# The gate of a modulation in a two-block mixer: sums on VectorE in place of matmuls

## The chip, the core and the metric

The kernel runs on one core of a Trainium2 chip. Its engines are TensorE (PE; its weight loads are listed as PEld), VectorE (DVE), ScalarE (ACT), GpSimd (POOL) and SyncE (SP), whose queue issues most DMAs. Each engine works through its own row of instructions in order and waits on semaphores for the others. The metric is the device time of one execution in microseconds. Of the kernel before there are three runs: 3599.32, 3597.35 and 3597.96 us, the median 3597.96.

## The reference, cut to what matters

Two blocks follow each other over 512 tokens of width D = 2048. The first one starts with a modulation of its input by a vector `c` and ends with a gate; between them are an attention and a state-space scan (SSD) over 512 tokens and 256 context tokens, which share one input projection `w_in`.

```
shift, scale, gate = split(silu(c) @ w_mod + b_mod, 3)        # w_mod: 2048 x 6144
px = (rmsnorm(x) * (1 + scale) + shift) @ w_in                 # the context likewise, from c_ctx
...                                                            # attention, scan, norms
x = x + gate * (merged @ w_out)
```

The context is not updated, so of its own modulation only shift and scale are used; the gate third of `w_mod` (2048 x 2048, 16 MB in fp32) is needed for `c` alone. The gate is first read when the output projection `w_out` is added to x, long after the scan. Everything is fp32 to the outside.

## The kernel before

**Main product.** An activation and a weight are each split in a high and a low half (fp32r), and a product is the sum of three matmuls, high-high, low-high, high-low. `weights` loads a `raw` tile of two rows of 128 (three buffers), `split` makes `wh` on ScalarE (a cast) and `wl` on VectorE (a subtraction), each with two buffers, and `block` runs the matmuls into PSUM tiles `acc`. A step is one such pair of rows; a product over D has eight steps.

**Stages of the first block.** `block1` loads c and c_ctx, makes `cs` (silu of both in the first 2 of 32 columns, per row of 128), then shift and scale by `mod`, in which `cs` is the stationary operand and a tile `wm` of 512 columns of `w_mod` streams; the two column groups of 512 and the two parities of k go to four different groups of 32 PSUM partitions. `sel` then sums them and puts the result on partitions. `ssd` runs four groups g (`ssd_group`): the columns of x (`xa`, `xb`, `xc`; 256 columns of `w_in`), of B and C (`ba`, `ca`, `bc`; 128 and 128), the convolution (`conv3`, tiles `P`, `u`, `uB`, `uC`), the states S and four chunks of the scan (`A`, `E`, `W`, `y`). `gate_half` is called after groups 1 and 2; it calls `mod` for two strips of 512 gate columns each, with 32 loads of 256 KB in a pool of two buffers per tag (`ss2`), and adds the bias. `keys` follows in the same pools, and then `heads`.

**What sets the order.** The code is written in the order of the computation; a scheduler with a timeline of its own sets each engine's row. `weights` stands under a high priority (`ahead` = 4000 in this stage), so steps of the main product are drawn forward between the other work; the gate's instructions have the ordinary priority and fill in. All DMAs named here are issued by SP in one row. A load into a pool's buffer is issued only when the last reader of that buffer is done, and what stands behind it in SP's row waits too.

Of the kernel before, what the change touches and what calls it, by code (L numbers as in the profile page):

```python
# [8 lines left out]
F32 = mybir.dt.float32  # L9
# [3 lines left out]
ALU = mybir.AluOpType  # L13
# [4 lines left out]
D = 2048  # L18
NX = 512
NCTX = 256  # L20
KT = 16
# [72 lines left out]
class Kernel:  # L94
# [171 lines left out]
    def block1(self):  # L266
        tc, nc, a = self.tc, self.nc, self.a
# [3 lines left out]
        wm = a["w_mod"][0]  # L271
# [6 lines left out]
        cs = [self.four(F32).rearrange("p j (s t) -> p (j s) t", s=2)]  # L278
        with self.pool("lead", 1) as lead, self.pool("lead2", 2) as lead2, self.pool("lead3", LX) as lead3, self.pool("wm", LM) as wmp:
# [10 lines left out]
            ps = self.psm()  # L290
# [1 line left out]
            cc = self.t(lead, [128, 32], F32, "cc")  # L292
            self.act(cc, ps[:, 0:32], AF.Tanh, scale=0.5)
            self.ts(cc, cc, 0.5, ALU.mult, 0.5, ALU.add)
            self.cs = self.t(self.b1, [128, KT, 32], F32, "cs")
            nc.vector.memset(self.cs, 0.0)
            self.tt(self.cs[:, :, 0:2], cc.rearrange("p (s k) -> p k s", s=2),
                    ps[:, 0:32].rearrange("p (s k) -> p k s", s=2), ALU.mult)
            s = self.t(lead, [128, 6, 4], F32, "s")


            for i in range(6):
                for q in range(4):
# [3 lines left out]
                    ps = self.psm()  # L307
# [22 lines left out]
            ps = self.psm()  # L330
            self.spread(ps, r[:, 0:4], 4)
            nc.vector.tensor_copy(rx[:, 0:NX], ps)
            ps = self.psm()
# [17 lines left out]
            for fg in range(4):  # L351
                m = ahead.pop()
                h4, e4, l4 = self.four(F32R), self.four(F32R), self.four(F32R)
                for j in range(4):
                    k = fg * 4 + j
                    sc = self.t(lead2, [128, 2], F32, "sc")
                    sh = self.t(lead2, [128, 2], F32, "sh")
                    q = self.q1["b_mod"]
                    self.ts(sh, m[:, j, 0:2], self.p1[:, q + k:q + k + 1], ALU.add)
                    self.ts(sc, m[:, j, 2:4], self.p1[:, q + KT + k:q + KT + k + 1], ALU.add, 1.0, ALU.add)  # L360
                    q = self.q1["norm_g"]
# [52 lines left out]
    def ssd(self):  # L414
        tc, nc, a = self.tc, self.nc, self.a
        w_in = a["w_in"][0]
        self.ysd = self.t(self.dr, [8, 128, NX], F32, "ysd")
        opx = self.zx
        opc = self.zc
        with ExitStack() as es:  # L420
            p1 = es.enter_context(self.pool("ssc", 1))

            dtT = self.t(p1, [128, 6, 64], F32, "dtT")
            ath = self.t(p1, [128, 6, 32], F32, "ath")
            atl = self.t(p1, [128, 6, 32], F32, "atl")
            ex = self.t(p1, [128, 6, 96], F32, "ex")
            wd = self.t(p1, [128, 6, 32], F32, "wd")
            dsk = self.t(p1, [128, 16], F32, "dsk")
            nc.sync.dma_start(out=dsk, in_=a["d_skip"][0:1, :].to_broadcast([128, 16]))
            pp = es.enter_context(self.pool("pp", 4))  # L430
            xa, xb, ba, ca, xc, bc = self.p0
            first = [self.padded(pp, xa, xc[:, 0:256]), self.padded(pp, xb, xc[:, 256:512]),
                     self.padded(pp, ba, bc[:, 0:256]), self.padded(pp, ca, None)]
            self.psum_pools(4, 4)
            with self.pool("dt", 1) as pd:
                w = self.dtw
                bias = self.t(pd, [32, 2], F32, "dtb")
                for i, (n, m) in enumerate((("dt_bias_f", "a_log_f"), ("dt_bias_b", "a_log_b"))):
                    nc.sync.dma_start(out=bias[i * 16:i * 16 + 16, 0:1], in_=a[n][0].rearrange("(h o) -> h o", o=1))
                    nc.sync.dma_start(out=bias[i * 16:i * 16 + 16, 1:2], in_=a[m][0].rearrange("(h o) -> h o", o=1))  # L440
                pre = self.t(pd, [32, NX + NCTX], F32, "dtpre")
                for ops, at, n in ((opx, 0, NX), (opc, NX, NCTX)):
                    ps = self.acc()
                    for k in range(KT):
                        self.mm(ps[0:64, 0:n], w[:, k, :], ops[k][0], start=(k == 0), stop=False)
                        self.mm(ps[0:64, 0:n], w[:, k, :], ops[k][1], start=False, stop=(k == KT - 1))
                    self.act(pre[:, at:at + n], ps[0:32, 0:n], AF.Identity, bias=bias[:, 0:1])
                    self.tt(pre[:, at:at + n], pre[:, at:at + n], ps[32:64, 0:n], ALU.add)
                st = self.t(pd, [64, NX + NCTX], F32, "dtst")
                self.softplus(pd, st[0:32, :], pre)  # L450
                self.act(bias[:, 1:2], bias[:, 1:2], AF.Exp)
                self.ts(st[32:64, :], st[0:32, :], bias[:, 1:2], ALU.mult, -1.0, ALU.mult)
                for i in range(2):
                    ps = self.psm()
                    for j in range(3):
                        tk = (i * 3 + j) * 128
                        self.tr(ps[:, j * 64:j * 64 + 64], st[:, tk:tk + 128])
                    nc.vector.tensor_copy(dtT[:, i * 3:i * 3 + 3, :], ps[:, 0:192].rearrange("p (j f) -> p j f", j=3))
                atr = self.t(pd, [128, 6, 32], F32R, "atr")
                nc.vector.tensor_copy(atr, dtT[:, :, 32:64])  # L460
                nc.vector.tensor_copy(ath, atr.bitcast(F32))
            self.dt_pool.__exit__(None, None, None)
            self.tt(atl, dtT[:, :, 32:64], ath, ALU.subtract)
            for i in range(2):
                ps = self.psm()
                for j in range(3):
                    t = i * 3 + j
                    o = j * 96
                    self.mm(ps[:, o:o + 16], self.le, dtT[:, t, 32:48])
                    self.mm(ps[:, o + 16:o + 32], self.ge, dtT[:, t, 48:64])  # L470
                    self.mm(ps[:, o + 32:o + 48], self.gt, dtT[:, t, 32:48])
                    self.mm(ps[:, o + 48:o + 64], self.lt, dtT[:, t, 48:64])
                    self.mm(ps[:, o + 64:o + 96], self.ones, dtT[:, t, 32:64])
                self.act(ex[:, i * 3:i * 3 + 3, :], ps[:, 0:288].rearrange("p (j f) -> p j f", j=3), AF.Exp)
            self.tt(wd, dtT[:, :, 0:32], ex[:, :, 32:64], ALU.mult)
            q = self.q1["conv_w0"]
            self.ts(self.p1[:, q:q + 64], self.p1[:, q:q + 64], 0.5, ALU.mult)
            with self.pool("ss1", 1) as s1, self.pool("ss2", 2) as s2, self.pool("ss4", 3) as self.p4:
                for g in range(4):
                    self.ssd_group(g, first if g == 0 else None, pp, s1, s2, dtT, ath, atl, ex, wd, dsk)  # L480
                    if g in (1, 2):
                        self.gate_half(g - 1, s1, s2)
                self.keys(pp)


# [173 lines left out]
            nc.scalar.copy(t[:, 0:512], vs[i])  # L659
            nc.sync.dma_start(out=self.vd[2 * i:2 * i + 2].rearrange("i p c -> p i c"), in_=t[:, 0:512].rearrange("p (i c) -> p i c", i=2))  # L660

    def gate_half(self, fg, pool, raws):
        q = self.q1["b_mod"] + 32
        m = self.mod(self.a["w_mod"][0], pool, [2 * D + fg * 1024, 2 * D + fg * 1024 + 512], raws, 1, self.nc.sync)
        for i in range(2):
            o = fg * 8 + i * 4
            self.tt(self.gate[:, o:o + 4], m[:, :, 2 * i], self.p1[:, q + o:q + o + 4], ALU.add)

    def heads(self):
        tc, nc, a = self.tc, self.nc, self.a  # L670
# [1198 lines left out]
```

## Time and profile before

| what | value |
|---|---|
| profiled execution | 3597.96 us |
| its span, first to last instruction | 3596.1 us |
| mean granted TensorE clock | 0.985 of full speed |
| PE busy | 3507.5 us (98%) |
| DVE busy | 2173.8 us (60%) |
| ACT busy | 1368.8 us (38%) |
| mean DMA rate | 123 GB/s |

The gate's matmuls lie between 262 and 523 us from the start of the span. A group of the page names a line, an engine, an operation and what it writes and reads (`acc<-wm,cs` is a matmul into `acc` from `wm` and `cs`). Lines of helpers (L112 for every matmul, L122 for every operation of two tensors, L132 for the fused multiply-add) stand for many places, so the tile names tell them apart. A matmul with fp32 operands leaves two records.

### The profile page before, as it was taken

The page shows a single profiled execution, that of the slowest core. Times are in us where ns is not written, and L with a number is a line of the kernel's source. Part 1 is how long each engine was busy: PE and PEld are TensorE (multiplying, and loading weights), DVE is VectorE, ACT ScalarE, POOL GpSimd, SP SyncE. Part 2 cuts the span into 40 slices and gives each one's busy share as a digit, 9 for nine tenths or more (in the row PEclk, how much of TensorE's full clock was granted, in tenths as well). Part 3 has the DMA queues.
Part 4 walks back from the last instruction along what each step waited for, and adds up shares of the span by engine and source line. Part 5 has one row for each costly group of instructions (what it writes and reads, how often), then busy time and mean ns, then how long its engine had stood idle before and what let it go on. Part 6 is the DMA issues. An engine that isn't in the chain of part 4 may idle for free.

```text
span 3596.1 us, 48583 instructions
## 1 busy us (share of the span) xinstructions
PE 3507.5 (98%) x18850; PEld 2748.8 (76%) x18850; DVE 2173.8 (60%) x3432; ACT 1368.8 (38%) x2225; POOL 55.7 (2%) x50
## 2 busy tenths in 40 slices
PE   6899999999999999999999998999999999999998
PEld 3486668777778788788877786888888888788887
DVE  3364555456554545675466557777788788555445
ACT  3333443356533323443233334444444444322212
POOL 0000000000000000000000000000000000000000
PEclk8999999999999999999999999999999999999999
DMA  8813333322144353334444443334443344534333
GB/s 278 283 36 112 99 100 88 95 67 82 48 138 147 107 149 109 112 116 116 132 121 129 145 141 129 117 117 127 131 122 107 118 123 141 187 122 126 99 100 106
DMA packets 352602, 442.22 MB, mean 123 GB/s; under 512 B 45871, under 2 KB 200179, under 8 KB 351731
## 3 DMA queue, kind: packets, MB, share of 16 engines
q1 hardware_dynamic: 349456, 437.82, 39.9%
q8 instruction: 148, 2.42, 0.3%
q10 hardware_dynamic: 2915, 1.29, 0.1%
q14 instruction: 83, 0.68, 0.1%
HBM read 383.45 MB, written 55.57 MB: 122 GB/s over the span
## 4 chain that ended last, share of the span: by engine, by line
PE 93%; DMA 3%; DVE 2%; ACT 1%; issue 0%; SPq 0%; POOL 0%; DVEq 0%; ACTq 0%; POOLq 0%
PE acc L112 44%; PE psm L112 23%; PE pp L112 23%; PE psm L116 2%; DMA wm<-in_w_mod_dram 1%; PE pt L116 1%; DVE wl L122 0%; DMA xr<-in_x_dram 0%; DMA raw<-in_ffn_w_down_dram 0%; DMA ym<-ysd 0%; DVE op L122 0%; PE acc L116 0%; DMA xr<-in_ctx_dram 0%; DMA fr<-in_ffn_w_up_dram 0%; DVE s L122 0%
## 5 line engine op out<-in xcount | busy, mean ns | idle before, releaser
L112 PE MATMUL acc<-op,wh 128*128 128x512 f32 (+2 forms) x4160 | 1254.5, 390 | 14.8 <-DVE sl L132 4.6
L112 PEld LDWEIGHTS acc<-op,wh 128*128 128x128 f32 (+1 forms) x4160 | 764.1, 189 | 229.5 <-issue 54.9
L122 DVE TENSOR_TENSOR wl<-raw,wh 128x512 fp32r<-128x512 f32 (+4 forms) x464 | 421.0, 908 | 690.0 <-ACT wh L136 641.1
L112 PE MATMUL acc<-op,wl 128*128 128x512 f32 (+2 forms) x2080 | 773.0, 389 | 2.1 <-DVE wl L122 2.1
L136 ACT CAST wh<-raw 128x512 fp32r<-128x512 f32 (+4 forms) x464 | 369.1, 796 | 1028.3 <-PE acc L112 637.7
L112 PE MATMUL pp<-wh,op 128*128 128x512 f32 x2112 | 529.9, 393 | 10.2 <-ACT wh L136 10.1
L136 ACT CAST wh<-fr 128x1024 fp32r<-128x1024 f32 x308 | 323.1, 1052 | 402.0 <-PE pp L112 350.2
L112 PEld LDWEIGHTS acc<-op,wl 128*128 128x128 f32 (+1 forms) x2080 | 390.4, 189 | 108.7 <-issue 26.9
L112 PEld LDWEIGHTS pp<-wh,op 128*128 128x128 f32 x2112 | 397.4, 188 | 99.3 <-ACT wh L136 10.7
L122 DVE TENSOR_TENSOR wl<-fr,wh 128x1024 fp32r<-128x1024 f32 x308 | 371.1, 1220 | 100.5 <-ACT wh L136 65.5
L112 PE MATMUL psm<-wh,op 128*128 128x512 f32 x1280 | 396.2, 391 | 7.3 <-DVE facc L122 7.3
L112 PEld LDWEIGHTS psm<-wh,op 128*128 128x128 f32 x1280 | 241.4, 189 | 58.2 <-issue 7.7
L112 PE MATMUL pp<-wl,op 128*128 128x512 f32 x1056 | 285.3, 392 | 0.2 <-DVE wl L122 0.2
L112 PE MATMUL psm<-wl,op 128*128 128x512 f32 x640 | 250.1, 391 | 0.3 <-DVE wl L122 0.3
L122 DVE TENSOR_TENSOR fr<-fr,fr 128x1024 f32<-128x1024 f32 x176 | 211.1, 1220 | 50.9 <-DMA fr<-in_ffn_w_gate_dram 33.0
L112 PEld LDWEIGHTS pp<-wl,op 128*128 128x128 f32 x1056 | 197.9, 188 | 43.6 <-DVE wl L122 0.6
L122 DVE TENSOR_TENSOR facc<-facc,psm 128x512 f32<-128x512 f32 x176 | 118.0, 686 | 60.6 <-PE psm L112 54.2
L112 PEld LDWEIGHTS psm<-wl,op 128*128 128x128 f32 x640 | 120.7, 189 | 25.7 <-DVE wl L122 0.7
L112 PE MATMUL acc<-wm,cs 128*32 128x512 f32 x384 | 126.1, 616 | 11.8 <-DMA wm<-in_w_mod_dram 11.8
L112 PE MATMUL acc<-wh,op 128*128 128x256 f32 x576 | 114.8, 293 | 0.0
L112 PEld LDWEIGHTS acc<-wh,op 128*128 128x128 f32 x576 | 91.9, 192 | 5.2 <-issue 3.8
L112 PE MATMUL pp<-wh,opx 128*128 128x512 f32 x352 | 93.8, 399 | 0.0
(469 smaller groups left out, 3506.0 us busy)
## 6 DMA issues: line engine op xcount, KB each, us to landing
raw<-in_w_in_dram SPq DMA_DIRECT2D x216, 256.0 KB, 2.8
fr<-in_ffn_w_gate_dram SPq DMA_DIRECT2D x88, 512.0 KB, 4.1
fr<-in_ffn_w_up_dram SPq DMA_DIRECT2D x88, 512.0 KB, 4.0
raw<-in_ffn_w_down_dram SPq DMA_DIRECT2D x88, 512.0 KB, 3.8
wm<-in_w_mod_dram SPq DMA_DIRECT2D x64, 512.0 KB, 5.8
raw<-in_w_out_dram SPq DMA_DIRECT2D x64, 512.0 KB, 3.8
raw<-in_w_in_dram SPq DMA_DIRECT2D x240, 128.0 KB, 2.4
wm<-in_w_mod_dram SPq DMA_DIRECT2D x64, 256.0 KB, 2.8
```

The source lines that it names most:

```text
L112: self.nc.tensor.matmul(out, lhsT=l, rhs=r, start=start, stop=stop, skip_group_check=more)
L116: self.nc.tensor.transpose(out, x, self.ident[0:n, 0:n])
L122: (e or self.nc.vector).tensor_tensor(out=out, in0=x, in1=y, op=op)
L136: self.nc.scalar.copy(h, x)
```

## The change

The gate third is no longer multiplied on TensorE. `gate_part(i)` makes one strip of 512 gate columns and is called after each of the four groups of the scan. Per row of 128 (k = 0 to 15) it loads a `wm` tile of 128x512 and multiplies it on VectorE by the silu of c for that row, a scalar per partition (`cv`), adding to an accumulator `ga` in SBUF: the first by `tensor_scalar`, fifteen by `scalar_tensor_tensor`. Then four matmuls with `ga` as the stationary operand and a column of ones sum over the 128 partitions, which also puts the result on partitions, and the bias is added straight from PSUM. `cs` moves to the pool of the leading stage, and `cv` (16 columns) stays in its place; the `wm` tiles have a pool `gw` of their own, with two buffers as before.

```diff
-            self.cs = self.t(self.b1, [128, KT, 32], F32, "cs")
+            self.cs = self.t(lead, [128, KT, 32], F32, "cs")
+            self.cv = self.t(self.b1, [128, KT], F32, "cv")
...
+            nc.vector.tensor_copy(self.cv, self.cs[:, :, 0])
...
-            with self.pool("ss1", 1) as s1, self.pool("ss2", 2) as s2, self.pool("ss4", 3) as self.p4:
+            with self.pool("ss1", 1) as s1, self.pool("ss2", 2) as s2, self.pool("ss4", 3) as self.p4, self.pool("gw", 2) as gw:
                 for g in range(4):
                     self.ssd_group(g, first if g == 0 else None, pp, s1, s2, dtT, ath, atl, ex, wd, dsk)
-                    if g in (1, 2):
-                        self.gate_half(g - 1, s1, s2)
+                    self.gate_part(g, s1, gw)
...
-    def gate_half(self, fg, pool, raws):
+    def gate_part(self, i, pool, raws):
+        nc = self.nc
         q = self.q1["b_mod"] + 32
-        m = self.mod(self.a["w_mod"][0], pool, [2 * D + fg * 1024, 2 * D + fg * 1024 + 512], raws, 1, self.nc.sync)
-        for i in range(2):
-            o = fg * 8 + i * 4
-            self.tt(self.gate[:, o:o + 4], m[:, :, 2 * i], self.p1[:, q + o:q + o + 4], ALU.add)
+        acc = self.t(pool, [128, 512], F32, "ga")
+        c0 = 2 * D + i * 512
+        for k in range(KT):
+            w = self.t(raws, [128, 512], F32, "wm")
+            nc.sync.dma_start(out=w, in_=self.a["w_mod"][0][k * 128:(k + 1) * 128, c0:c0 + 512])
+            s = self.cv[:, k:k + 1]
+            if k == 0:
+                self.ts(acc, w, s, ALU.mult)
+            else:
+                self.stt(acc, w, s, acc, ALU.mult, ALU.add)
+        ps = self.psm()
+        for j in range(4):
+            self.mm(ps[:, j:j + 1], acc[:, j * 128:j * 128 + 128], self.ones[:, 0:1])
+        o = i * 4
+        self.tt(self.gate[:, o:o + 4], ps[:, 0:4], self.p1[:, q + o:q + o + 4], ALU.add)
```

The scheduler lays the rows anew from the second gate load on to the first heads (PE's rows agree again from there to the end). Numbers of tiles differ between the two kernels, since they count all tiles made: `wl_2084` before is `wl_2144` now, 60 later. Three places:

VectorE in the first group of the scan, before: the low halves `wl`, `wd` and `XW` of the scan, the additions in `W`.

```order
L122 TENSOR_TENSOR W_1681<-le_1324,dtT_1345 128x512
L122 TENSOR_TENSOR W_1681<-W_1681,y_1682 128x512
L122 TENSOR_TENSOR wd_1349<-dtT_1345,ex_1348 128x192
L122 TENSOR_TENSOR wl_2084<-raw_2081,wh_2083 128x2x256
L122 TENSOR_TENSOR XW_1610<-XB_1545,wd_1349 128x256 x2
L122 TENSOR_TENSOR wl_2167<-raw_2163,wh_2166 128x2x256
```

The same place now (of the products 1880 to 1898, seven in a row, two stand):

```order
L127 TENSOR_SCALAR ga_1873<-wm_1874,cv_117 128x512
L122 TENSOR_TENSOR W_1686<-W_1686,y_1687 128x512
L132 SCALAR_TENSOR_TENSOR ga_1873<-wm_1877,cv_117,ga_1873 128x512
L132 SCALAR_TENSOR_TENSOR ga_1873<-wm_1880,cv_117,ga_1873 128x512
...
L132 SCALAR_TENSOR_TENSOR ga_1873<-wm_1898,cv_117,ga_1873 128x512
L122 TENSOR_TENSOR wd_1351<-dtT_1347,ex_1350 128x192
L132 SCALAR_TENSOR_TENSOR ga_1873<-wm_1901,cv_117,ga_1873 128x512
L132 SCALAR_TENSOR_TENSOR ga_1873<-wm_1904,cv_117,ga_1873 128x512
L122 TENSOR_TENSOR wl_2144<-raw_2141,wh_2143 128x2x256
L132 SCALAR_TENSOR_TENSOR ga_1873<-wm_1907,cv_117,ga_1873 128x512
```

The first product stands ahead of the addition in `W`, ten more between that addition and the low half that came two rows behind it.

VectorE at the second strip, now, from the low half of the last wide step of group 1 on; `P` copies belong to the next group's convolution:

```order
L122 TENSOR_TENSOR wl_2991<-raw_2988,wh_2990 128x2x256
L132 SCALAR_TENSOR_TENSOR ga_2720<-wm_2727,cv_117,ga_2720 128x512
L132 SCALAR_TENSOR_TENSOR ga_2720<-wm_2730,cv_117,ga_2720 128x512
L122 TENSOR_TENSOR XW_2462<-XB_2183,wd_1351 128x256 x2
L132 SCALAR_TENSOR_TENSOR ga_2720<-wm_2733,cv_117,ga_2720 128x512
L132 SCALAR_TENSOR_TENSOR ga_2720<-wm_2736,cv_117,ga_2720 128x512
L122 TENSOR_TENSOR wl_3074<-raw_3070,wh_3073 128x2x256
L132 SCALAR_TENSOR_TENSOR ga_2720<-wm_2739,cv_117,ga_2720 128x512
L132 SCALAR_TENSOR_TENSOR ga_2720<-wm_2742,cv_117,ga_2720 128x512
L132 SCALAR_TENSOR_TENSOR ga_2720<-wm_2745,cv_117,ga_2720 128x512
L505 COPY P_3018<-acc_2777 128x256
```

Two or three products stand between two low halves; further on in the strip one or two, between the 769-column operations of the convolution.

SP in the first group, before, loads of 128-column pieces (two DMAs each) and the third gate load:

```order
L146 DMA raw_2188<-in_w_in_dram 128x2x128 x2
L146 DMA raw_2213<-in_w_in_dram 128x2x128 x2
L146 DMA raw_2238<-in_w_in_dram 128x2x128 x2
L146 DMA raw_2263<-in_w_in_dram 128x2x128 x2
L949 DMA wm_2667<-in_w_mod_dram 128x512
L146 DMA raw_2288<-in_w_in_dram 128x2x128 x2
```

and now (of eleven gate loads in a row, three stand):

```order
L146 DMA raw_2248<-in_w_in_dram 128x2x128 x2
L671 DMA wm_1880<-in_w_mod_dram 128x512
L671 DMA wm_1883<-in_w_mod_dram 128x512
...
L671 DMA wm_1910<-in_w_mod_dram 128x512
L146 DMA raw_2273<-in_w_in_dram 128x2x128 x2
L671 DMA wm_1913<-in_w_mod_dram 128x512
```

Eleven gate loads, each waiting for a buffer, stand where one load of the main product followed the other.

## Rows read from the trace of the kernel before

**Rows 1.** The page's busy shares by engine, and its chain by engine.

```profile
PE 3507.5 (98%) x18850; PEld 2748.8 (76%) x18850; DVE 2173.8 (60%) x3432; ACT 1368.8 (38%) x2225; POOL 55.7 (2%) x50
PE 93%; DMA 3%; DVE 2%; ACT 1%; issue 0%; SPq 0%; POOL 0%; DVEq 0%; ACTq 0%; POOLq 0%
```

**Rows 2.** Busy time by stretch: the gate's stretch, then one without gate matmuls.

```profile
core 0: us, PE busy (x) PEld busy (x) DVE busy (x) ACT busy (x) POOL busy (x), PEclk, DMA share, GB/s
254.00:523.00 269.00, 269.00 (x1198) 173.19 (x1196) 140.84 (x292) 100.32 (x261) 0.00 (x0) 1.00 0.36 104
523.00:600.00 77.00, 77.00 (x488) 67.11 (x487) 46.83 (x96) 37.99 (x107) 0.00 (x0) 1.00 0.23 63
```

**Rows 3.** Groups of PE in 254 to 523 us: the gate's matmuls (busy, mean ns).

```profile
L112 PE MATMUL acc<-wm,cs 128*32 128x512 f32 x128 | 63.8, 605 | 0.0
```

**Rows 4.** Timeline of PE: start, duration, instruction; main product, single gate matmuls, two together.

```profile
308.02 0.39 PE L112 MATMUL acc<-op,wl 128*128 128x512 f32 x1
308.25 0.62 PE L112 MATMUL acc<-op,wh 128*128 128x512 f32 x2
...
302.94 1.04 PE L112 MATMUL acc<-wm,cs 128*32 128x512 f32 x2
303.92 0.38 PE L112 MATMUL acc<-op,wl 128*128 128x256 f32 x1
...
290.42 1.05 PE L112 MATMUL acc<-wm,cs 128*32 128x512 f32 x4
```

**Rows 5.** Waits in 260 to 620 us: all engines, then SP's queue (total, times, longest).

```profile
ACT wh L136 <- PE acc L112: 116.7, 33, 7.0
...
SPq L949 <- PE acc L112: 143.2, 55, 5.5
SPq L146 <- DVE wl L122: 92.1, 27, 7.9
```

**Rows 6.** Timeline of PE: two small matmuls after each other.

```profile
237.18 0.39 PE L112 MATMUL psm<-dtT,ones 128*128 128x32 f32 x2
237.40 0.37 PE L112 MATMUL psm<-dtT,le 128*128 128x16 f32 x2
```

**Rows 7.** DVE: groups in 254 to 523 us, then two starts from the timeline.

```profile
L122 DVE TENSOR_TENSOR XW<-XB,wd 128x256 f32<-128x256 f32 x28 | 10.8, 419 | 19.1 <-ACT XB L530 10.3 <-PE psm L112 8.9
L132 DVE SCALAR_TENSOR_TENSOR u<-P,p,u 128x769 f32<-128x769 f32 x12 | 11.7, 1014 | 0.0
L132 DVE SCALAR_TENSOR_TENSOR uC<-P,p,uC 128x512 f32<-128x512 f32 x4 | 3.0, 742 | 0.0
...
304.15 0.74 DVE L132 SCALAR_TENSOR_TENSOR uC<-P,p,uC 128x512 f32<-128x512 f32 x1
304.82 0.68 DVE L122 TENSOR_TENSOR E<-E,W 128x512 f32<-128x512 f32 x1
```

**Rows 8.** DMA: gate loads (KB, median us to landing), their spread, lead-stage loads.

```profile
wm<-in_w_mod_dram SPq DMA_DIRECT2D x62, 256.0 KB, 2.7
DMA to landing us min/median/max: 2.6/2.7/3.2
...
wm<-in_w_mod_dram SPq DMA_DIRECT2D x64, 512.0 KB, 5.8
```

**Rows 9.** Timeline where strip 1 comes to stand: DVE, then PE.

```profile
233.28 0.69 DVE L122 TENSOR_TENSOR W<-W,y 128x512 f32<-128x512 f32 x1
243.66 0.36 DVE L122 TENSOR_TENSOR wd<-dtT,ex 128x192 f32<-128x192 f32 x1 [9.69 <-ACT ex L119]
246.31 0.69 DVE L122 TENSOR_TENSOR wl<-raw,wh 128x512 fp32r<-128x512 f32 x1 [2.29 <-ACT wh L136]
...
250.38 0.40 PE L112 MATMUL acc<-op,wl 128*128 128x512 f32 x1
```

**Rows 10.** Busy time by stretch: the granted clock (before the DMA share).

```profile
238.00:249.00 11.00, 11.00 (x51) 10.42 (x51) 1.05 (x2) 2.16 (x6) 0.00 (x0) 0.53 0.07 17
```

## The prediction

> **What bounds the kernel now.** I read the page's busy shares and its chain first: TensorE (PE) is busy 98% of the span and makes up 93% of the chain that ended last [rows 1]. A share over the whole span says nothing on one stage, so next I cut out the stage that the change touches. The gate's matmuls run from 262 to 523 us; in 254 to 523 us PE is busy all of the 269.00 us, at full clock, while VectorE (DVE) works 140.84 us, ScalarE 100.32 us, and the DMA share is 0.36 [rows 2]. Then the groups of that stretch: 128 records (64 matmuls, two records each) of `acc<-wm,cs` hold 63.8 us [rows 3]. "Busy" may hide pipelining, so I read the timeline for pitches, start to start. A 128x512 matmul of the main product follows its neighbour after 0.23 us (308.02, 308.25), so the main work goes at its usual pitch with no hole. A gate matmul at 302.94 holds PE until 303.92: 0.98 us [rows 4]. Last the waits: DMA issues of `wm` waited 143.2 us for PE, and the high half `wh` on ScalarE 116.7 us for PE [rows 5]. Everything waits for PE, PE for nothing. So in this stretch a microsecond taken from PE is one from the kernel, as long as nobody else becomes late.
>
> **The change part by part.** The profiled execution took 3597.96 us, 1.86 over its span of 3596.1, and is itself the median of the three runs; I count from it.
>
> (a) Removed from PE: the 64 gate matmuls. In the timeline of the stretch they stand in 61 places: 58 alone, as at 302.94, and three times two together (290.42, four records, 1.05 us) [rows 4]. The 61 pitches lie at 0.97 or 0.98, so 61 x 0.977 = 59.6 us. Also gone are the eight `sel` matmuls of 4 columns and, on ScalarE, two row copies. Small matmuls of this kind stand 0.22 apart (237.18 to 237.40) [rows 6]; 8 x 0.22 = 1.8 us.
>
> A rule of the Trainium skill speaks against so full a price. "Perfetto Trace Analysis", section Identifying the Most-Contended Engine, says that matmul busy share is no measure of headroom and that the share of weight loads is; by that, 173.19 of 269 us [rows 2] would leave a third of PE free, and an estimate by that page has only two thirds of the 59.6 us come back, 39 us; the sum below would end near 3573 us. The pitches of [rows 4] speak for the full price, and I keep it.
>
> (b) Added to PE: 16 matmuls with a column of ones, 16 x 0.22 = 3.5 us by the same row. PE's sum: 59.6 + 1.8 - 3.5 = 57.9 us less.
>
> (c) Added to DVE: 64 products on 128x512, 60 of them fused multiply-adds. The nearest row is the `uC` one, 742 ns, starting 0.67 us before the next instruction (304.15 to 304.82) [rows 7]. 64 x 0.67 = 43 us. With 140.84 us now in the stretch [rows 2] that is 184 us in 269 - 58 = 211 us, 87%: it fits, with little to spare. The four additions of 4 columns take the place of four like them, and the copies of 16 columns become one instead of two; I take 0 for these.
>
> (d) Moved: who waits for the gate's loads. Their number and size stay (64 of 256 KB), but DVE is now the engine that waits, and it runs its row in order; behind it are the low halves `wl`, without which PE stops at the third matmul of a step. `gw` has two buffers: a load lands 2.7 us after its issue [rows 8], its product takes 0.67, and only then can the load after next be issued. So two loads per 2.7 + 0.67 + about 0.1 = 3.45 us. The loads also stand in SP's queue in front of the main product's `raw` loads; three `raw` buffers are ahead of that.
>
> Strip 1 by the order: after the addition at 233.28 [rows 9] come nine products that wait on landings, and then `wl_2144`, the one that stood as `wl_2084` at 246.31. The first of these landings follows a release at 233.75: five rounds of 3.45 from there give 251.0, and the subtraction of 0.69 ends near 252.0 instead of 247.0. PE first reads it at 250.38 [rows 9]: 1.6 us of stall. That row also gives the cushion, 250.38 - 247.0 = 3.4 us, which a low half has before PE needs it.
>
> Strip 2, from `wl_2991` to `wl_3174`: DVE's row holds 11 products (7.4 us), five subtractions (3.1), twelve operations on 256 columns (4.1, at 419 ns less the overlap) and eight on 769 (6.6, at up to 1014) [rows 7]: 21.2 us. Its first seven products are paced by landings, 3.5 x 3.45 = 12.1 us against 7.3 us of work there, so add 4.8: 26.0 us. PE's matmuls between the same two points, at 0.23 us per 512 columns and half that for 256, with the small ones between, come to 20.6 us. DVE falls 5.4 us back, the cushion takes 3.4, 2.0 are left; as some low halves are already late when the strip begins, I take 3. Strips 3 and 4 have the same loads, fewer wide operations beside them, and steps of 3.5 to 5.9 us of PE: counted likewise some 4.7 us of lag each, 1.3 past the cushion; I take 2 each. Strips: 1.6 + 3 + 2 + 2 = 8.6 us. Bounds: 0 (PE's row has other work ahead) and, with landings of 3.2 us, the longest of this size [rows 8], 7 rounds x 0.5 x 4 strips = 14 more, 22.6.
>
> (e) Between the strips lie the chunks of the scan, whose steps go from ScalarE to PE to DVE and back. With PE's gate matmuls gone they have less cover. From 523 to 600 us there are chunks and no gate matmuls, and PE is busy 77.00 of 77.00 us [rows 2]: cover enough. Bounds 0 and 8 us; I take 3.
>
> Sum: 57.9 - 8.6 - 3 = 46.3 us. 3597.96 - 46.3 = **3552 us**. What comes after the scan keeps its order and simply starts earlier.
>
> **The rivals.**
> 1. All covered: the strips' waits fit under PE's row and the cushion. For it: PE waits for nothing now, and a cushion of 3.4 us stands at each step. Against it: the counts of strips 2 to 4. 3597.96 - 57.9 = 3540 us.
> 2. The clock falls in the strips. The stretch 238 to 249 us was granted 0.53, nearly all of it the lower of the two levels (1.2 GHz), after a run of tiny matmuls [rows 10]; that fall cost 11 x 0.47 = 5.2 us. If each strip's stalls bring one such fall, 4 x 5.2 = 21 us: 3573 us. Against it: the stalls counted here are 1 to 3 us, and PE works at its usual pitch between them. The Trainium skill's "TensorE: Matmul & The Clock Gate", section HAM oscillation, describes this: waits for DMA between bursts of matmuls, after each of which the next begins at the low clock.
> 3. Slower, by landing time. Per strip 14 loads go in 7 rounds, so each microsecond on the landing costs 7 us per strip, 28 in all. From 2.7 + 46.3/28 = 4.3 us on, the change loses. The 512 KB loads of the lead stage take 5.8 us [rows 8]: 3552 + 28 x 3.1 = 3639 us. For it: the loads come in bursts, 256 KB per 1.73 us, about 150 GB/s beside the `raw` loads. Against it: same size, same queue, and 62 of them landed within 2.6 to 3.2 us.
> 4. No change: PE was not the bound here and the freed time turns into waits for DVE, whose 184 us of work are then stretched over the old 269 us. 3598 us. Against it: the waits of [rows 5].
>
> **How the numbers follow.** Forecast 0.60, all covered 0.22, clock 0.09, no change 0.04, slower 0.05. The range: downward to rival 1 with 3 us for its uncertainty, 3537; upward the strips' upper bound, 14 us, and (e)'s, 5 us, give 3571, and part of rival 2 lies up to 3575. 3537 to 3575. Differences of 0.2% (7 us) are about what a measurement can tell from none. Faster: forecast, rivals 1 and 2, 0.91; same 0.04; slower 0.05.
>
> **What would show it.** No `acc<-wm,cs` after 200 us; `ga<-wm,cv,ga` 60 times on DVE near 0.74 us; four idle places of DVE that end with `wm` landings; PE waits for DVE `wl` of 5 to 20 us in all between 245 and 560 us; the end of the keys about 46 us earlier; the same spans from there on. I am wrong in the first step if PE's busy time in the scan falls by much less than 58 us, in the fourth if `wm` lands later than 3.2 us or PE's waits for `wl` pass 20 us.

## The result and the profile after

The changed kernel took 3532.42 us (median of four runs, 3526.77 to 3536.14), the kernel before beside it 3597.65 us; the ratio is 0.9817, its 95% interval 0.98 to 0.9835. That is 65 us less where 46 were forecast, below the lower end of the range (3537). The profiled execution took 3531.79 us with a span of 3530.0.

Two lines of the page of the changed kernel, busy shares and chain by engine, answer [rows 1]:

```profile
PE 3438.7 (97%) x18738; PEld 2740.7 (78%) x18738; DVE 2213.8 (63%) x3495; ACT 1367.9 (39%) x2223; POOL 55.1 (2%) x50
PE 90%; DMA 5%; DVE 3%; issue 1%; ACT 1%; SPq 0%; POOL 0%; DVEq 0%; POOLq 0%; ACTq 0%
```

PE's busy time fell by 68.8 us, VectorE's rose by 40.0, and in the chain the shares of DMA (3 to 5%) and VectorE (2 to 3%) have grown. Busy time by stretch, changed kernel (engines with their instruction counts, then the granted clock, the DMA share and GB/s), answers [rows 2]:

```profile
250.00:300.00 50.00, 48.02 (x242) 38.86 (x241) 34.62 (x71) 19.31 (x47) 0.00 (x0) 1.00 0.34 96
300.00:350.00 50.00, 49.97 (x291) 42.08 (x291) 37.70 (x75) 25.29 (x68) 0.00 (x0) 1.00 0.38 106
350.00:400.00 50.00, 48.76 (x258) 40.47 (x257) 40.31 (x87) 25.59 (x67) 0.00 (x0) 1.00 0.33 93
400.00:450.00 50.00, 50.00 (x281) 42.25 (x280) 40.86 (x75) 18.44 (x45) 0.00 (x0) 1.00 0.52 148
...
500.00:550.00 50.00, 46.92 (x341) 42.43 (x339) 33.83 (x68) 19.71 (x54) 0.00 (x0) 1.00 0.41 125
```

PE has short holes in three of these stretches, VectorE is busy 68 to 82% in them all, and the granted clock stays 1.00. The gate's tile `wm` (count, then shortest, median and longest ns, first and last start; below, the idle time of VectorE before it with the times, and the landing in us) answers [rows 7] and [rows 8]:

```profile
L132 DVE SCALAR_TENSOR_TENSOR ga<-wm,cv,ga x60: 740/750/754, 234.1 to 526.7; 128x512 f32<-128x512 f32 x60
...
  DMA wm<-in_w_mod_dram: 39.0, 36
...
DMA to landing us min/median/max: 2.6/2.9/3.3
```

VectorE stands 39.0 us before landings. PE's own waits in 234 to 634 us (total, times, longest), where before it had 0.2 us in the whole scan:

```profile
PE acc L112 <- DVE wl L122: 4.1, 4, 1.2
PE psm L112 <- DVE XW L122: 2.1, 2, 1.7
PE psm L112 <- DMA kr<-kd: 0.6, 1, 0.6
PE psm L112 <- DVE y L122: 0.2, 1, 0.2
```

7.0 us in all; in two more traces of the changed kernel (`again` and `again2` below) it is 5.2 and 5.8, 6.0 in the mean. To see where the rest went, I cut the span by instructions that every kernel has: the first small matmul that reads `dtT` (the start of the scan's four groups), the first that reads `KH` (the heads), the first `ym` (block 1's merge), the first `fin` (second block), the first cast of `fr` (its feed-forward), the last sum into `facc`. Views by tile, changed kernel (x count: ns; first and last start):

```profile
L112 PE MATMUL psm<-dtT,le x12: 178/263/374, 234.1 to 241.3; 128*128 128x16 f32 x12
...
L112 PE MATMUL psm<-KH,op x160: 221/280/622, 633.9 to 915.9; 128*128 128x256 f32 x128, 128*128 128x128 f32 x32
...
L132 DVE SCALAR_TENSOR_TENSOR ym<-ym,p,R x8: 744/751/753, 953.8 to 975.3; 128x512 f32<-128x512 f32 x8
...
L119 ACT ACTIVATE fin<-yt x6: 631/632/635, 1409.9 to 1956.9; 128x512 f32<-128x512 f32 x6
...
L136 ACT CAST wh<-fr x308: 1030/1052/1064, 2154.4 to 3015.9; 128x1024 fp32r<-128x1024 f32 x154
...
L122 DVE TENSOR_TENSOR facc<-facc,psm x176: 674/686/690, 3044.3 to 3521.2; 128x512 f32<-128x512 f32 x176
```

So the scan takes 633.9 - 234.1 = 399.8 us; before, 694.3 - 234.1 = 460.2. The same for every kernel of this study (us; one trace each, the last column the median of the timed runs):

| kernel | start | scan | heads | to `fin` | `fin` to `fr` | to the end | whole |
|---|---|---|---|---|---|---|---|
| before | 234.1 | 460.2 | 321.6 | 456.3 | 747.3 | 1367.7 | 3597.65 |
| before2 | 231.5 | 460.2 | 321.5 | 455.4 | 746.2 | 1366.4 | 3594.51 |
| changed | 234.1 | 399.8 | 319.9 | 456.1 | 744.5 | 1366.8 | 3532.42 |
| again | 234.5 | 398.7 | 320.5 | 456.4 | 745.8 | 1367.1 | 3532.27 |
| again2 | 230.7 | 398.5 | 320.4 | 456.4 | 744.4 | 1367.5 | 3532.33 |
| prio200 | 235.0 | 398.3 | 320.5 | 455.1 | 747.4 | 1366.6 | 3530.08 |
| prio1000 | 231.2 | 396.7 | 318.9 | 455.9 | 744.0 | 1367.6 | 3524.89 |
| pre | 231.6 | 394.9 | 320.5 | 454.7 | 746.2 | 1365.9 | 3524.84 |
| preprio | 230.1 | 394.7 | 320.4 | 456.4 | 747.3 | 1365.5 | 3525.71 |
| noload | 232.8 | 388.7 | 321.4 | 456.0 | 757.7 | 1367.4 | 3534.70 |
| none | 232.4 | 400.9 | 321.5 | 456.5 | 759.2 | 1368.7 | 3549.24 |
| nodve | 231.7 | 404.4 | 320.5 | 456.1 | 755.6 | 1368.8 | 3551.01 |
| thin | 233.3 | 395.7 | 320.4 | 456.7 | 756.3 | 1366.5 | 3536.38 |
| dve2 | 229.9 | 395.6 | 319.3 | 450.5 | 772.7 | 1365.7 | 3544.02 |
| gw1 | 233.5 | 401.6 | 318.8 | 456.0 | 759.0 | 1364.3 | 3543.52 |
| pool2 | 233.7 | 396.7 | 321.8 | 455.4 | 754.0 | 1366.9 | 3539.59 |
| pair2 | 232.0 | 431.8 | 320.0 | 455.4 | 754.9 | 1367.5 | 3575.32 |

Two readings come before any experiment's own. The start differs by 2.6 us between two traces of one kernel (before and before2), so it carries scatter. And the stretch from `fin` to `fr` falls in two sorts: 744 to 747 us in the nine traces of kernels whose PE row there is the one of before, 754 to 773 us in the eight others, whose PE row the scheduler laid anew in the second block although the edit stands in the first. The whole time of those eight can't be compared with the changed kernel; their scan can. One of the four executions of `noload` took 8317.87 us and is left out of its ratio; the other three lie between 3531.27 and 3534.76 us.

### The profile page after: what moved, and what is told of

Read it like the earlier page. It is cut to its first block, busy times and chain, and to the rows that moved or that the text cites. A ratio compares the mean times of both kernels' runs of the same rounds, so it can differ in the third digit from the quotient of the medians.

```text
span 3530.0 us, 48454 instructions
## 1 busy us (share of the span) xinstructions
PE 3438.7 (97%) x18738; PEld 2740.7 (78%) x18738; DVE 2213.8 (63%) x3495; ACT 1367.9 (39%) x2223; POOL 55.1 (2%) x50
## 4 chain that ended last, share of the span: by engine, by line
PE 90%; DMA 5%; DVE 3%; issue 1%; ACT 1%; SPq 0%; POOL 0%; DVEq 0%; POOLq 0%; ACTq 0%
PE acc L112 41%; PE psm L112 23%; PE pp L112 23%; DMA wm<-in_w_mod_dram 2%; PE psm L116 2%; DVE wl L122 1%; PE pt L116 1%; DMA xr<-in_x_dram 0%; DMA raw<-in_ffn_w_down_dram 0%; DVE ga L132 0%; DMA ym<-ysd 0%; DMA fr<-in_ffn_w_gate_dram 0%; DVE op L122 0%; DMA xr<-in_ctx_dram 0%; DMA fr<-in_ffn_w_up_dram 0%
## 5 line engine op out<-in xcount | busy, mean ns | idle before, releaser
L112 PE MATMUL pp<-wh,op 128*128 128x512 f32 x2112 | 529.7, 393 | 10.1 <-ACT wh L136 10.1
L112 PE MATMUL acc<-wl,op 128*128 128x256 f32 x288 | 84.4, 294 | 1.0 <-DVE wl L122 0.9
```

The source lines that it names most:

```text
L112: self.nc.tensor.matmul(out, lhsT=l, rhs=r, start=start, stop=stop, skip_group_check=more)
```

## The experiments

**What the gate cost on TensorE: none, nodve, noload.** `none` is the kernel before with `gate_half` cut down to its loads, `nodve` the changed kernel with `gate_part` cut down in the same way, `noload` the kernel before without the loads too. In each a memset takes the place of the gate, as here in `noload`:

```diff
-        m = self.mod(self.a["w_mod"][0], pool, [2 * D + fg * 1024, 2 * D + fg * 1024 + 512], raws, 1, self.nc.sync)
...
+        self.nc.vector.memset(self.gate[:, fg * 8:fg * 8 + 8], 1.0)
```

> The kernel before without the gate's arithmetic: the 64 loads stay, the 64 gate matmuls, the eight sums over partitions and the two row copies are left out, and the gate is set to 1. It prices the whole gate on TensorE. Theory A: a gate matmul costs more than its own pitch of 0.98 us, since the matmul behind it takes 0.29 us in the mean where its neighbours take 0.20; 61 places at 1.07 to 1.08 us and 1.8 us of small matmuls give 67 to 68 us, so 3530 us, and 5 us less, 3525, if what appears after the scan comes with it. Theory B, the forecast's prices, 61.4 us: 3536 us, and then the changed kernel, which still has 3.5 us of matmuls with a column of ones, would stand below it or level with it.

> The changed kernel without the arithmetic of its strips: the 64 loads stay in four strips of 16, the 64 products on VectorE and the 16 matmuls with the column of ones are left out, and the gate is set to 1. Against the changed kernel it prices the strips. Theory A, as the trace of the changed kernel reads: waits of TensorE for VectorE of 7 us in the strips and 3 us of small matmuls go, so some 10 us less, 3522 us, and level with the kernel that leaves the gate out of the old order. Theory B, strips that cost nothing since TensorE has other work: 3 to 4 us less, 3529 us. The forecast's 8.6 + 3 + 3.5 us would give 3517 us.

Measured: 3549.24 us (ratio to before 0.9864, 0.985 to 0.9877) and 3551.01 us (0.9875, 0.9861 to 0.9889). Both are slower than the changed kernel that computes the gate, and no theory had that. Two causes stand in the table: 10 to 14 us in the second block's new row, and a scan that is no shorter than the changed kernel's. Busy time by stretch in `nodve`:

```profile
250.00:300.00 50.00, 39.94 (x169) 31.59 (x168) 20.34 (x46) 8.67 (x15) 0.00 (x0) 0.86 0.69 209
```

and its waits in 233 to 640 us:

```profile
PE acc L112 <- ACT wh L136: 12.1, 5, 5.2
...
ACT wh L136 <- DMA raw<-in_w_in_dram: 34.5, 5, 8.5
```

With no arithmetic behind them the gate's loads come in a burst (209 GB/s), the main product's `raw` loads land late, and PE, waiting for high halves, is busy 39.94 of 50 us at a granted clock of 0.86. In `none` it is the same with less: 44.47 of 50 us at 0.91. The two kernels price that burst, not the gate. Hence a third:

> The kernel before without anything of the gate: its 64 loads, its 64 matmuls, the sums over partitions and the row copies are left out, and the gate is set to 1. Of the runs so far the two that left the arithmetic out but kept the loads let these come in a burst, and TensorE then waited 8 to 12 us for the main product's high halves; this one has no burst, so the start of the keys' matmuls (the first matmul that reads KH, at 694.1 us before and 633.9 us in the changed kernel) gives the price of the gate on TensorE alone. Theory A, gate matmuls that also slow the matmul behind them: 59.5 + 1.8 + 8.4 = 69.7 us, so 624 us, 9 to 10 us earlier than in the changed kernel. Theory B, the forecast's price: 61.4 us, 633 us, level with the changed kernel. The time of the whole says less: after this stage the scheduler lays the second block's rows anew, as in those two, and there 14 us were lost; with that 3537 us by A and 3546 us by B.

Measured: a scan of 388.7 us, the heads' first matmul at 621.5 us. The whole took 3534.70 us (0.9831, 0.9814 to 0.9847), after 757.7 us from `fin` to `fr`. PE's only wait in the scan (232 to 622 us):

```profile
PE psm L112 <- DMA kr<-kd: 1.9, 1, 1.9
```

So the gate held the scan 460.2 - 388.7 = 71.5 us before: theory A, and 10 us above the forecast's 61.4. PE's busy time in the scan falls from 459.89 to 386.75 us, by 73.1 us, and the granted clock in 228 to 256 us, where it dips, is 0.82 in both, so neither waits nor the clock make up the difference. Why can be seen at one gate matmul of the kernel before. Timeline of PE (start, duration), with the one at 302.94 of [rows 4] between the first line and the others:

```profile
302.62 0.40 PE L112 MATMUL acc<-op,wh 128*128 128x256 f32 x2
...
304.14 0.28 PE L112 MATMUL acc<-op,wh 128*128 128x256 f32 x1
304.26 0.38 PE L112 MATMUL psm<-uC,uB 128*128 128x128 f32 x2
```

and of its weight loads (PEld) in the same place:

```profile
302.94 0.14 PEld L112 LDWEIGHTS acc<-wm,cs 128*32 128x32 f32 x2
303.92 0.19 PEld L112 LDWEIGHTS acc<-op,wl 128*128 128x128 f32 x1 [0.84 <-issue]
304.03 0.19 PEld L112 LDWEIGHTS acc<-op,wh 128*128 128x128 f32 x1
```

The load for 304.14 starts at 304.03, beside the matmul before it; that pair stands at the usual pitch of 0.12 us for 256 columns (304.14 to 304.26). At both borders of the gate matmul the load starts only with its own matmul. The matmul behind (303.92 to 304.14) takes 0.22 in place of 0.12, and the two ahead (302.62 to 302.94) take 0.32 in place of 0.24. That is 0.18 us per place beside its 0.977: 61 x 0.18 = 11.0, and 59.6 + 1.8 + 11.0 = 72.4 against 71.5 measured (73.1 by PE's busy time). The other places show the same: against the median pitch of its kind between 254 and 523 us the record ahead takes 0.08 to 0.10 us more at 57 of the 61 and the one behind 0.10 to 0.11 more at 53, and at all 61 the loads at both borders start within 0.01 us of their own matmuls. That the late loads are the cause is read from this coincidence; no run changes them alone. The Trainium skill's "TensorE: Matmul & The Clock Gate", Part 3: Packing small matmuls, says in its list of what overlaps that a weight load overlaps a running matmul only where the row groups differ. By that line no load here would overlap, since all of them use all rows. The same section also lets a load into the background weight buffer be pulled ahead, and no row here shows which buffer a load goes to. The trace agrees with the line at the two borders of the gate matmul, and not inside the main product, where the load at 304.03 stands beside the matmul of 303.92.

**What the strips cost: thin, dve2, gw1.**

```diff
 thin
-                self.stt(acc, w, s, acc, ALU.mult, ALU.add)
+                self.stt(acc[:, 0:32], w[:, 0:32], s, acc[:, 0:32], ALU.mult, ALU.add)
 dve2
+            self.stt(w, w, s, w, ALU.mult, ALU.add)
 gw1
-            with ..., self.pool("gw", 2) as gw:
+            with ..., self.pool("gw", 1) as gw:
```

> The changed kernel with fused multiply-adds on 32 of the 512 columns (the first product of a strip stays whole, so the gate is wrong in the other columns): loads, buffers, order of waits and matmuls stay, but some 60 x 0.6 = 36 us of work on VectorE go. Read at the first matmul that reads KH, 633.9 us in the changed kernel. Theory A, the strips' waits of TensorE (7.0 us there) come from the landings for which VectorE waits: they stay within 2 us, 632 to 635 us. Theory B, they come from VectorE being full: they go, 627 us.

> The changed kernel with a second fused multiply-add per gate load, in place on the load's tile and read by nobody: 64 more operations of 0.67 us, 43 us more on VectorE, and each load's buffer is held 0.67 us longer. Theory A (VectorE has little to spare, 87% in the stretch by the forecast): most of the 43 us beyond the room left come back as waits of TensorE for the low halves, 20 to 35 us, so 3552 to 3567 us. Theory B (the row of TensorE has other work and VectorE was waiting for landings in the strips anyway): under 10 us, below 3542 us.

> The changed kernel with one buffer for the gate's loads in place of two: each load is issued only when the product before it is done, so a round of one load takes 2.9 us of landing, 0.75 of product and some 0.1, 3.7 us, and 16 of them 60 us a strip, 240 us in all, against 300 us of the stretch. Theory A, the forecast's third rival (landings on VectorE's path set the strips): 7 rounds more per strip past the cushion, some 2 us each, 40 to 60 us more, 3570 to 3600 us. Theory B (VectorE's row has slack, other work stands between the products): under 15 us more, below 3547 us.

Measured, scan: 395.7, 395.6 and 401.6 us, against 398.5 to 399.8 in three traces of the changed kernel (whole: 3536.38 us, 0.9838, 0.9823 to 0.9853; 3544.02 us, 0.9852, 0.9839 to 0.9866; 3543.52 us, 0.9859, 0.9843 to 0.9876; the second block's row is a new one in all three). VectorE's idle time before the strips' operations (tile `ga`) in `thin`:

```profile
  DMA wm<-in_w_mod_dram: 51.0, 42
```

in `dve2`:

```profile
  DMA wm<-in_w_mod_dram: 13.0, 20
```

and in `gw1`:

```profile
  DMA wm<-in_w_mod_dram: 69.0, 42
```

Taking VectorE's work away lengthens its waiting for landings from 39.0 to 51.0 us; doubling it shortens the waiting to 13.0. The second product runs in time that VectorE spent waiting for the next load: 43 us more of work, and the scan is not longer. "VectorE has little to spare" falls. With one buffer it waits 69.0 us, 30 more, and the scan is 2 to 3 us longer, where the forecast's third rival would have 40 to 60: that rival falls as well, since the scheduler puts other work between the products and PE's row has other matmuls. `thin` came out between its theories (heads' first matmul at 629.0 us). `dve2` has the shorter scan with the more work; its row in the scan is another one too, so an order alone seems to move the scan by 3 to 4 us, which this run doesn't separate from the work.

**Whether the place decides: prio200, prio1000, pre, preprio.** These keep the second block's row, so their whole time counts.

```diff
 prio200 (prio1000: with 1000)
-                    self.gate_part(g, s1, gw)
+                    with self.tc.high_priority(200):
+                        self.gate_part(g, s1, gw)
 pre (preprio: this with priority 1000)
-                    self.ssd_group(g, ...)
                     self.gate_part(g, s1, gw)
+                    self.ssd_group(g, ...)
```

> The changed kernel with the strips' instructions under a small priority (200), which moves only a few products by one or two places, mainly in the last strip; the rows of the second block stay. By either theory 3532 us within 2; a larger difference would say that single places in the order are worth microseconds.

> The changed kernel with the strips' instructions under a larger priority (1000): products move by up to four places on VectorE, the addition behind the strip's matmuls and the loads come sooner; the rows of the second block stay. Theory A (waits at places that the order decides): within 3 us of 3532 in either direction, with the waits of TensorE for low halves in other places. Theory B (VectorE's work itself is the price): 3532 us and waits of 7 us as before.

> The changed kernel with each strip called before its group of the scan in place of after it: the same instructions, and the rows of the second block stay as they are in the changed kernel, so that the whole time can be compared here. The last two strips then stand a group earlier, and the last chunks of the scan, where TensorE waited about 3 us between 500 and 550 us, have none beside them. Theory A, the strips' cost (11 us against a kernel without gate) is waits at places that the order decides: 2 to 6 us less than the changed kernel, 3527 to 3530 us. Theory B, the waits go with the strips wherever they stand: 3532 us within 2.

> The changed kernel with each strip called before its group of the scan and its instructions under the priority 1000: both edits that shortened the scan in single traces (394.9 and 396.7 us from the first small matmul that reads dtT to the first that reads KH, 399.8 and 398.7 in the changed kernel), with the rows of the second block as they are. If those were the order: 392 to 396 us, and a time 4 to 7 us below that of the changed kernel beside it. If they were scatter: 398 to 400 us and no difference that can be told.

Measured: 3530.08 us (0.982, 0.9807 to 0.9834), 3524.89 (0.9812, 0.9799 to 0.9825), 3524.84 (0.9813, 0.9799 to 0.9826), and `preprio` 3525.71 (0.9811, 0.9797 to 0.9824) beside a changed kernel of 3532.33 (`again2`, 0.9827, 0.9814 to 0.984). In the scan `pre` and `preprio` take 394.9 and 394.7 us, some 4 less than the changed kernel. All of PE's waits in `preprio`, 230 to 625 us:

```profile
PE acc L112 <- DVE wl L122: 2.2, 2, 1.9
PE psm L112 <- ACT A L599: 0.2, 1, 0.2
```

2.4 us in place of 6.0 in the mean of the changed kernel's three traces, and the scan shorter by about as much: in `preprio` the strips' waits went with their places in the order. `pre` supports this less than its time suggests. It still waits 4.8 us (`prio1000` 4.5), and the dip of the clock at the head of the scan cost it less: the granted clock in 228 to 256 us is 0.88 in `pre`, 0.82 in the changed kernel, 0.78 in `preprio`. That the two scans agree to 0.2 us is therefore in part luck. In the whole the intervals of `preprio` and `again2` overlap; the medians differ by 6.6 us, of which the traces give 4 to the scan. The other three ran beside a kernel before of 3592.99 us, so against the changed kernel only their ratios count, and those lie within its interval. `pre`, `prio1000` and `preprio` have the lowest times that were measured, level with each other; that they beat the changed kernel is likely and not shown by the whole time.

**Other places for the sums: pool2, pair2.** `pool2` puts the arithmetic on GpSimd, `pair2` leaves the gate on PE (from the kernel before), two column groups side by side:

```diff
 pool2
-                self.ts(acc, w, s, ALU.mult)
+                self.ts(acc, w, s, ALU.mult, e=nc.gpsimd)
...
-                self.stt(acc, w, s, acc, ALU.mult, ALU.add)
+                self.ts(w, w, s, ALU.mult, e=nc.gpsimd)
+                self.tt(acc, w, acc, ALU.add, nc.gpsimd)
 pair2
...
+                w = self.t(raws, [128, 2, 256], F32, "wm")
+                nc.sync.dma_start(out=w, in_=src[h])
+                for i in range(2):
+                    g = 32 * (i + 2 * h)
+                    self.mm(ps[g:g + 32, 0:256], self.cs[:, k, :], w[:, i, :], k == 0, k == KT - 1)
...
```

> The changed kernel with the strips' arithmetic on GpSimd, as a multiplication in place and an addition (124 operations on 128x512 and four that start a strip). VectorE's row is then as in the kernel without gate, and TensorE keeps the 16 matmuls with a column of ones. Read from the first small matmul of the scan (reads dtT) to the first matmul that reads KH, 399.8 us in the changed kernel and 388.7 us without gate. Theory A (VectorE's in-order row is what TensorE waits for): 392 to 394 us. Theory B (GpSimd and VectorE slow each other, or the sums come too late): 400 us or more. The whole time is only comparable up to the second block, whose rows are laid anew.

> The kernel before with the gate kept on TensorE, but each load made of 256 columns of both strips, whose two matmuls of 256 columns go next to each other to different groups of 32 columns of the array; four such groups hold four quarters of 1024 gate columns, and the sums over parities go. In the lead stage matmuls that stood so side by side cost half of one alone (128 of 512 columns held 62 us). Theory A: 64 pairs of 0.5 us and 0.1 to 0.15 us for the matmul behind each, 38 to 42 us in place of 68: the first matmul that reads KH comes at 666 us (694.1 before). Theory B: the two of a pair do not overlap, 694 us or later.

Measured: `pool2` a scan of 396.7 us, between the theories (3539.59 us, 0.9851, 0.9838 to 0.9865, new row in the second block). `pair2` has its heads' first matmul at 663.8 us (expected 666) and a scan of 431.8, 28.4 less than before (3575.32 us, 0.9949, 0.9934 to 0.9964): theory A. Timeline of PE in `pair2`, three matmuls of 256 columns side by side (six records), then one alone (two):

```profile
304.75 0.63 PE L112 MATMUL acc<-wm,cs 128*32 128x256 f32 x6
305.31 0.50 PE L112 MATMUL psm<-A,ltr 128*128 128x512 f32 x1
305.74 0.62 PE L112 MATMUL acc<-wm,cs 128*32 128x256 f32 x2
306.28 0.39 PE L112 MATMUL acc<-op,wh 128*128 128x256 f32 x1
```

Behind the three the next matmul comes after 0.56 us, behind the one after 0.54: side by side, the second and third are almost free. So laid out the gate would have given back 28 of the 71.5 us without VectorE.

**What appears behind the scan: again, before2, again2.** The same kernels once more, unaltered.

> The changed kernel once more, unaltered, for its scatter and for a second trace. Four runs of it so far lie between 3526.8 and 3536.1 us. In its trace VectorE starts the same instruction 60.4 us earlier than before at the end of the keys and 66 us earlier at the end of the kernel. Theory A: the 5 to 6 us that appear after the scan, where the rows are the same, are a difference between single executions; then this trace, laid beside the first one of the changed kernel, drifts by several microseconds after the scan too, or the time moves by as much. Theory B: they belong to the change; then the drift is the same within 1 us and the time is 3532 us within 3.

> The kernel before once more, for a second trace and more runs. From the first matmul that reads KH to the last sum into facc there are 2892.9 us in its first trace and 2887.3 and 2889.8 us in the two of the changed kernel, though the rows of that part are the same. Theory A (scatter of single executions): this trace gives a figure that differs from 2892.9 by 2 us or more, or the two kernels' figures overlap. Theory B (the change shortens that part): 2893 us within 1.

> The changed kernel once more beside the next one and the kernel before. Theory A and B as for the kernel before: from the first matmul that reads KH to the last sum into facc 2887 to 2890 us by either. The time 3532 us within 3, and a start of the scan's small matmuls between 230 and 235 us: this start has differed by up to 5 us between kernels whose rows up to there are the same.

Measured, from `KH` to the end: 2892.9 and 2889.5 us before, 2887.3, 2889.8 and 2888.7 us in the changed kernel. They overlap: theory A. (Whole: 3532.27, 0.9816, 0.9803 to 0.983; 3594.51, 1.0, 0.9991 to 1.0008; 3532.33.) Of the 5 us only some 1.3 repeat, all in the heads (321.6 and 321.5 against 319.9, 320.5 and 320.4); the others are differences of single executions.

## Why the prediction fell short, point by point

**What bounds.** Right: in the scan a microsecond off PE was one off the kernel, and more than was counted came back. The Trainium skill's "Perfetto Trace Analysis", section Identifying the Most-Contended Engine, says to judge TensorE's headroom by MFU (the arithmetic it does as a share of its peak) or by the share of weight loads. By the second of these the prediction's estimate was a third of PE free here and 39 us back of 59.6. The trace does not agree: 71.5 us came back for the gate's whole work on PE, so the pitches were nearer to it than the share of weight loads.

**(a) The gate matmuls: the mis-sized term.** Its own pitch, 0.977 us, was read rightly. The step "the 61 pitches lie at 0.97 or 0.98, so 61 x 0.977 = 59.6 us" took this for the whole price. The matmuls ahead and behind each pay 0.08 to 0.10 us; with them (a) is 71.5 us in place of 61.4, as `noload` measured. The row that shows it stood in [rows 4], one line below the gate matmul: its successor at 303.92 has 256 columns, and I did not read on to the start after it.

**(b) The ones:** 16 matmuls of 128x1, as forecast. In the timeline of PE they hold it 0.81, 0.81, 0.36 and three times 0.37 us, 3.1 us in all, where 3.5 was forecast; no run leaves them out alone.

**(c) VectorE:** the operation took 750 ns (forecast 0.74, each 0.67 apart). "87%: it fits, with little to spare" was too dark: 68 to 82% in the windows above, and 161.93 of the 211 us from 254 to 465 us (77%), since the strips reach beyond that stretch on both sides. `dve2` shows that even twice the work fits, since it runs while VectorE waits for loads.

**(d), (e) Stalls: too large.** Forecast 3.5 + 8.6 + 3 = 15.1 us for ones, strips and coupling; measured, as the changed kernel (mean of 399.8, 398.7 and 398.5 is 399.0) against `noload`, 10.3. Landing was nearly as counted (2.9 us in the median against 2.7, the longest 3.3), and the sign for the strips, 5 to 20 us of waits for `wl`, was missed: 4.1, 2.3 and 3.9 us in the three traces. Timeline of VectorE in the changed kernel at strips 1 and 4:

```profile
251.26 0.69 DVE L122 TENSOR_TENSOR wl<-raw,wh 128x512 fp32r<-128x512 f32 x1
...
512.67 0.75 DVE L132 SCALAR_TENSOR_TENSOR ga<-wm,cv,ga 128x512 f32<-128x512 f32 x1 [2.16 <-DMA wm<-in_w_mod_dram]
513.34 0.76 DVE L122 TENSOR_TENSOR XW<-XB,wd 128x256 f32<-128x256 f32 x2
```

and of PE:

```profile
259.34 0.50 PE L112 MATMUL acc<-op,wl 128*128 128x512 f32 x1 [1.24 <-DVE wl L122]
...
514.24 1.10 PE L112 MATMUL psm<-XW,XB 128*128 128x512 f32 x2 [1.68 <-DVE XW L122]
```

In strip 1 the low half starts at 251.26 and is done near 252.0, as forecast, but PE did not stall on it: it works without a hole from 249 to 258.10 us. Its holes come at later low halves, 1.24 us up to 259.34 and 0.74 up to 272.78, so that their sum, 2.0 us, agrees with the forecast's 1.6 by luck. Strip 2, for which I took the most (3), cost 1.2, as PE lacks in 350 to 400; strip 3 (2) cost nothing, PE being busy all of 400 to 450. Strip 4 (2), from 495 to 527 us, has 3.1 us of PE's holes in 500 to 550, and here the forecast's mechanism shows best: `XW` at 513.34 stands in VectorE's row behind a product that waited 2.16 us for its landing, and PE waits 1.68 us for it. By that this wait, too, belongs to the strips and not to (e), the coupling; `preprio`, whose strips stand a group earlier, has no wait for `XW`. What is left for (e) in the trace is 0.2 us for `y`, where 3 were taken.

Of the 10.3 us the ones' 3.1 and the waits, 6.0 in the mean less the 1.9 of `noload`, explain 7.2; the other 3.1 stay open.

**The sum.** -71.5 + 10.3 = -61.2 in the scan, where -61.4 + 15.1 = -46.3 was forecast: 14.9 us, 10.1 of them from (a), 4.8 from (b), (d) and (e). The rest, to the 65 us of the medians, is 1.3 us in the heads and scatter.

**Range and rivals.** The lower end rested on rival 1, "all covered", with 57.9 us as the most there was to win. It was no ceiling, because (a) had no bound of its own. That the strips cost something was right, so rival 1 was not what happened, though its time is nearer. Rival 2 didn't occur: the granted clock is 1.00 from 249 us on, and the dip to 0.54 in 238 to 249 us was there before (0.53). Rival 3 was overrated in its mechanism: `gw1` turned 30 us of added waiting into 2 to 3. Rival 4 fell with `noload`.

## What to carry to other kernels

Price a matmul that stands alone in a dense row from the start of its predecessor to the end of its successor's pitch, not by its own pitch: here a 32-column fp32 one cost 0.977 us plus 0.18 at its borders, nearly a fifth more. An engine that waits for loads in its row has idle time that more work can fill, so a high share of work is by itself no sign that others will wait for it: `dve2` added 43 us and the scan did not grow. Where a scheduler lays the rows, compare an experiment stage by stage, since an edit in one block cost 8 to 27 us in another that it did not touch; and try the place of an off-path job, and not its size alone.

## What was not expected of the hardware

GpSimd's work slowed VectorE. Groups of VectorE in the scan of `pool2` (busy, mean ns):

```profile
L122 DVE TENSOR_TENSOR wl<-raw,wh 128x512 fp32r<-128x512 f32 x82 | 66.1, 807 | 68.4 <-ACT wh L136 68.4
L122 DVE TENSOR_TENSOR XW<-XB,wd 128x256 f32<-128x256 f32 x40 | 22.7, 600 | 7.8 <-ACT XB L531 7.8
```

and of `noload`:

```profile
L122 DVE TENSOR_TENSOR wl<-raw,wh 128x512 fp32r<-128x512 f32 x82 | 56.5, 688 | 75.4 <-ACT wh L136 73.7 <-PE acc L112 1.4
L122 DVE TENSOR_TENSOR XW<-XB,wd 128x256 f32<-128x256 f32 x40 | 15.5, 418 | 10.5 <-ACT XB L530 7.2 <-PE psm L112 3.3
```

The same operations take 807 in place of 688 ns and 600 in place of 418 while GpSimd computes on tensors of 128x512 (1842 ns for a multiplication, 1455 for an addition in the mean). The Trainium skill's "GPSIMD Engine Reference", section Key points, says that the two engines share their interfaces to SBUF and contend where a VectorE instruction has two inputs there (or runs in a 2-port mode). The trace agrees: both groups have two such inputs, while `S<-S,psm`, with one input in PSUM, keeps its time (413 ns against 416 in `noload`). VectorE is busy 271.72 us in the scan of `pool2`, 271.80 in the changed kernel and 230.54 in `noload`. So the work moved off VectorE still took VectorE's time, and the gain stayed at 2 to 3 us.
